# Low-rank update kernel: A read as 24 rows of 2 KB and transposed on the chip, A and B issued first from ScalarE's queue

## The chip, the cores and the metric

The kernel runs on one core of a Trainium2 chip. The core has five engines with their own instruction streams: TensorE (PE, matmuls; its weight loads are shown as PEld), VectorE (DVE), ScalarE (ACT), GpSimd (POOL) and SyncE (SP), which here only issues transfers. Sixteen DMA engines move data between the chip's main memory and the core's on-chip memory; they serve the queues of all engines that issue transfers. The metric is the device time of one execution in microseconds (us), a median over runs.

## The reference

```python
batch, seq, d_model, r = 16, 512, 768, 16      # x: 16 x 512 x 768, float32
lora = np.matmul(np.matmul(x, A), B)           # A: 768 x 16, B: 16 x 768
return (x + scale * lora).astype(np.float32)   # scale = 0.5
```

Seen as a matrix, x has 8192 rows of 768 floats (25.2 MB). All of it is read once and an output of the same size is written once. A and B are 48 KB each.

## The kernel before

The 8192 rows are cut into six parts, `PARTS = [2, 6, 8, 16, 16, 16]`, counted in sub-tiles of 128 rows. Part i has a tile of its own, `x_sb{i}`, and is loaded by one transfer (line 69); all six tiles fit on the chip together, so no load waits for room. The text calls these loads x0 to x5. After x1, the loop issues A (line 71) and B (line 72). All eight transfers, and later all eight stores (line 136), are issued by SyncE, so they stand in one queue.

A is laid out in memory as 768 rows of 16 floats. The kernel wants it with 128 rows on the 128 partitions, in six groups (`a_mm`, 128 x 6 x 16), so the load takes 768 pieces of 64 bytes. VectorE casts A and B to 16-bit floats (lines 75 and 77). GpSimd makes a 128 x 128 identity matrix.

The work goes by chunks of at most four sub-tiles, 17 in all. For a chunk:

- `transposed(c, j)`, for each of six column blocks j: TensorE transposes the sub-tiles with the identity (line 94) and ScalarE copies the result out of PSUM as 16-bit floats (line 96, `xt_sb`).
- `projected(c)`: six matmuls of `a_mm` with the transposed blocks add up to x times A, transposed (line 103); VectorE scales and casts it (line 108, `yt_sb`).
- `added(c, subs)`: for each sub-tile two matmuls with `b_mm` (line 120, `lora_ps`), and VectorE adds the result to x in place (line 126).
- `finished(c)`: once a part, or half of a part for the last two, is done, it is stored (line 136).

The main loop works on chunk c's transposes and chunk c-1's additions in turn. The framework plans the order of each engine's instructions at build time with its own estimate of durations and arrivals, so TensorE's order can differ from the program's; it also sets all waits. A transfer that reuses a tile's memory waits until the readers of what was there are done.

Of the kernel before, what the change touches and what calls it, by code (L numbers as in the profile page):

```python
# [1 line left out]

# [6 lines left out]


MM_DT = mybir.dt.float16

PARTS = [2, 6, 8, 16, 16, 16]

STORES = {4: [8, 8], 5: [8, 8]}

CHUNK = 4


@with_exitstack  # L20
def kernel(
    ctx: ExitStack,
    tc: tile.TileContext,
    x: bass.AP,
    A: bass.AP,
    B: bass.AP,
    scale: bass.AP,
    out: bass.AP,
):

    nc = tc.nc
    fp32 = mybir.dt.float32
    P = 128

    x2 = x.flatten_outer_dims()
    out2 = out.flatten_outer_dims()
    T, D = x2.shape
    R = A.shape[1]  # L40
    ND = D // P
    assert D % P == 0 and sum(PARTS) * P == T
    n_splits = [(n0, min(512, D - n0)) for n0 in range(0, D, 512)]
    sc = float(scale)

    const = ctx.enter_context(tc.tile_pool(name="const", bufs=1))
    xpool = ctx.enter_context(tc.tile_pool(name="xp", bufs=1))
    xtpool = ctx.enter_context(tc.tile_pool(name="xtp", bufs=6))
    ypool = ctx.enter_context(tc.tile_pool(name="yp", bufs=2))
    ps_xt = ctx.enter_context(tc.tile_pool(name="ps_xt", bufs=3, space=bass.MemoryType.PSUM))  # L50
    ps_y = ctx.enter_context(tc.tile_pool(name="ps_y", bufs=1, space=bass.MemoryType.PSUM))
    ps_l = ctx.enter_context(tc.tile_pool(name="ps_l", bufs=2, space=bass.MemoryType.PSUM))


    parts = []
    tok = 0
    for i, S in enumerate(PARTS):
        x_sb = xpool.tile([P, S, D], fp32, name=f"x_sb{i}")
        parts.append((x_sb, tok, S))
        tok += S * P  # L60

    def rows(t2, i):
        _, tok0, S = parts[i]
        return t2[ds(tok0, S * P), :].rearrange("(p s) d -> p s d", s=S)

    a_f32 = const.tile([P, ND, R], fp32, name="a_f32")
    b_f32 = const.tile([R, D], fp32, name="b_f32")
    for i in range(len(parts)):
        nc.sync.dma_start(out=parts[i][0], in_=rows(x2, i))  # L69
        if i == 1:  # L70
            nc.sync.dma_start(out=a_f32, in_=A.rearrange("(c p) r -> p c r", p=P))
            nc.sync.dma_start(out=b_f32, in_=B)

    a_mm = const.tile([P, ND, R], MM_DT, name="a_mm")
    nc.vector.tensor_copy(out=a_mm, in_=a_f32)  # L75
    b_mm = const.tile([R, D], MM_DT, name="b_mm")
    nc.vector.tensor_copy(out=b_mm, in_=b_f32)  # L77

    ident = const.tile([P, P], fp32, name="ident")
    make_identity(nc, ident)  # L80


    chunks = [
        (i, s0, min(CHUNK, S - s0))
        for i, (_, _, S) in enumerate(parts)
        for s0 in range(0, S, CHUNK)
    ]
    state = {}

    def transposed(c, j):  # L90
        i, s0, n = chunks[c]
        xt_ps = ps_xt.tile([P, CHUNK, P], fp32, name="xt_ps")
        for s in range(n):
            nc.tensor.transpose(xt_ps[:, s, :], parts[i][0][:, s0 + s, ds(j * P, P)], ident)  # L94
        xt_sb = xtpool.tile([P, CHUNK * P], MM_DT, name="xt_sb")
        nc.scalar.copy(out=xt_sb[:, 0 : n * P], in_=xt_ps[:, 0:n, :])  # L96
        state[c, j] = xt_sb

    def projected(c):
        n = chunks[c][2] * P  # L100
        ps_yt = ps_y.tile([R, CHUNK * P], fp32, name="ps_yt")
        for j in range(ND):
            nc.tensor.matmul(  # L103
                ps_yt[:, 0:n], a_mm[:, j, :], state.pop((c, j))[:, 0:n],
                start=(j == 0), stop=(j == ND - 1),
            )
        yt_sb = ypool.tile([R, CHUNK * P], MM_DT, name="yt_sb")
        nc.vector.tensor_scalar(  # L108
            out=yt_sb[:, 0:n], in0=ps_yt[:, 0:n], scalar1=sc, scalar2=None,
            op0=mybir.AluOpType.mult,  # L110
        )
        state[c] = yt_sb

    def added(c, subs):
        i, s0, n = chunks[c]
        subs = [s for s in subs if s < n]
        lora = {s: ps_l.tile([P, D], fp32, name="lora_ps") for s in subs}
        for s in subs:
            for n0, w in n_splits:
                nc.tensor.matmul(  # L120
                    lora[s][:, ds(n0, w)], state[c][:, ds(s * P, P)], b_mm[:, ds(n0, w)],
                    start=True, stop=True,
                )
        for s in subs:
            xs = parts[i][0][:, s0 + s, :]
            nc.vector.tensor_tensor(out=xs, in0=xs, in1=lora[s], op=mybir.AluOpType.add)  # L126

    def finished(c):
        i, s0, n = chunks[c]
        del state[c]  # L130
        end = 0
        for w in STORES.get(i, [parts[i][2]]):
            end += w
            if end == s0 + n:
                piece = slice(end - w, end)
                nc.sync.dma_start(out=rows(out2, i)[:, piece, :], in_=parts[i][0][:, piece, :])

    for c in range(len(chunks)):
        for j in range(3):
            transposed(c, j)  # L140
        if c >= 1:
            added(c - 1, (0, 1))
        for j in range(3, ND):
            transposed(c, j)
        if c >= 1:
            added(c - 1, (2, 3))
            finished(c - 1)
        projected(c)
    c = len(chunks) - 1
    added(c, (0, 1))  # L150
    added(c, (2, 3))
    finished(c)


# [1 line left out]
_INS = ['x', 'A', 'B', 'scale']  # L156
_OUTS = [((16, 512, 768), 'float32')]

_NUMBERS = {'scale': 0.5}


# [26 lines left out]
```

## Time and profile before

| | |
|---|---|
| median of three timings | 125.4 us (125.14, 125.40, 125.58) |
| span of the profiled execution, first to last instruction | 123.5 us |
| the profiled execution's own total | not given by the profile; 1.6 to 2.1 us of the timings lie around the span |
| TensorE busy | 98.0 us |
| VectorE busy | 68.5 us |
| ScalarE busy | 52.5 us |
| GpSimd busy | 0.7 us |
| data queue q1 | 50.43 MB, 16 DMA engines busy 96.4% of the span |
| last store issued | 111.40 us, landing 11.3 us later |

A transfer "lands" when the last of the 16 DMA engines has written its share. In tables by stretch of time, a DMA share of 1.00 means that each of the 16 engines had one packet under way all the time; it can be over 1, for packets overlap within an engine. A large packet counts in full where it is booked, so very short stretches swing widely, and stretches of several microseconds are the ones to read.

### The profile page before, as it was taken

The page shows a single profiled execution, that of the slowest core. Times are in us where ns is not written, and L with a number is a line of the kernel's source. Part 1 is how long each engine was busy: PE and PEld are TensorE (multiplying, and loading weights), DVE is VectorE, ACT ScalarE, POOL GpSimd, SP SyncE. Part 2 cuts the span into 40 slices and gives each one's busy share as a digit, 9 for nine tenths or more (in the row PEclk, how much of TensorE's full clock was granted, in tenths as well). Part 3 has the DMA queues.
Part 4 walks back from the last instruction along what each step waited for, and adds up shares of the span by engine and source line. Part 5 has one row for each costly group of instructions (what it writes and reads, how often), then busy time and mean ns, then how long its engine had stood idle before and what let it go on. Part 6 is the DMA issues. An engine that isn't in the chain of part 4 may idle for free.

```text
span 123.5 us, 1607 instructions
## 1 busy us (share of the span) xinstructions
PE 98.0 (79%) x614; PEld 61.0 (49%) x614; DVE 68.5 (55%) x83; ACT 52.5 (42%) x103; POOL 0.7 (1%) x6
## 2 busy tenths in 40 slices
PE   0263999999958999999999999999999999730000
PEld 0253665565616675656665665747475656200000
DVE  0000253962887267577686868686868576890000
ACT  4060364375504573737364555556473737000000
POOL 2000000000000000000000000000000000000000
PEclk9999999999999999999999999999999999995555
DMA  4999999799799899989799999989989999999990
GB/s 109 426 454 380 422 533 430 334 499 477 302 493 493 366 416 483 446 350 493 275 408 456 443 422 504 430 382 493 403 366 438 414 454 422 424 435 422 446 390 32
DMA packets 2840, 50.54 MB, mean 409 GB/s; under 512 B 1024, under 2 KB 1024, under 8 KB 1296
## 3 DMA queue, kind: packets, MB, share of 16 engines
q1 hardware_dynamic: 2832, 50.43, 96.4%
q8 instruction: 5, 0.08, 0.2%
q14 instruction: 3, 0.02, 0.0%
HBM read 25.26 MB, written 25.17 MB: 408 GB/s over the span
## 4 chain that ended last, share of the span: by engine, by line
PE 72%; DMA 8%; DVE 7%; issue 1%; DVEq 1%; SPq 0%; ACT 0%; ACTq 0%
PE xt_ps L94 38%; PE lora_ps L120 18%; PE ps_yt L103 16%; DMA x_sb<-in_x_dram 8%; DVE x_sb L126 6%; DVE yt_sb L108 1%; DVEq L183 1%; SPq L69 0%; ACT xt_sb L96 0%; ACTq L96 0%
## 5 line engine op out<-in xcount | busy, mean ns | idle before, releaser
L96 ACT CAST xt_sb<-xt_ps 128x512 f16<-128x512 f32 (+1 forms) x102 | 51.2, 568 | 52.0 <-PE xt_ps L94 47.2
L126 DVE TENSOR_TENSOR x_sb<-x_sb,lora_ps 128x768 f32<-128x768 f32 x64 | 58.0, 951 | 23.5 <-PE lora_ps L120 23.5
L94 PE MATMUL xt_ps<-ident,x_sb 128*128 128x128 f32 x384 | 52.3, 288 | 8.4 <-DMA x_sb<-in_x_dram 8.3
L94 PEld LDWEIGHTS xt_ps<-ident,x_sb 128*128 128x128 f32 x384 | 43.7, 146 | 20.7 <-issue 13.9
L120 PE MATMUL lora_ps<-b_mm,yt_sb 16*128 16x512 f16 (+1 forms) x128 | 26.7, 323 | 3.8 <-DVE x_sb L126 2.2
L103 PE MATMUL ps_yt<-xt_sb,a_mm 128*16 128x512 f16 (+1 forms) x102 | 24.4, 375 | 0.0
L120 PEld LDWEIGHTS <-yt_sb 16*128 16x128 f16 x128 | 9.5, 92 | 15.1 <-issue 7.8
L108 DVE TENSOR_SCALAR yt_sb<-ps_yt 16x512 f16<-16x512 f32 (+1 forms) x17 | 10.9, 642 | 8.0 <-PE ps_yt L103 8.0
L103 PEld LDWEIGHTS <-a_mm 128*16 128x16 f16 x102 | 7.9, 91 | 13.0 <-issue 5.1
L75 DVE CAST a_mm<-a_f 128x96 f16<-128x96 f32 x1 | 0.2, 210 | 11.4 <-DMA a_f<-in_A_dram 11.4
L96 ACT ACT_TABLE_LOAD x1 | 1.3, 1283 | 0.7 <-PEq L169 0.7
L77 DVE CAST b_mm<-b_f 16x768 f16<-16x768 f32 x1 | 0.5, 537 | 0.0
masks.py:199 POOL TENSOR_SCALAR_AFFINE_SELECT ident<-ident 128x128 f32<-128x128 f32 x1 | 0.3, 294 | 0.1
masks.py:197 POOL MEMSET ident<- 128x128 f32 x1 | 0.2, 205 | 0.3 <-POOLq L169 0.3
L169 POOL MEMSET const-bfloat16-1.0<- 128x1 bf16 x1 | 0.1, 103 | 0.0
L169 POOL MEMSET const-uint8-127<- 128x1 uint8 x1 | 0.1, 103 | 0.0
L169 POOL MEMSET const-float32-0.0<- 128x1 f32 x1 | 0.1, 100 | 0.2 <-issue 0.2
L169 POOL MEMSET const-float32-1.0<- 128x1 f32 x1 | 0.1, 100 | 0.0
## 6 DMA issues: line engine op xcount, KB each, us to landing
x_sb<-in_x_dram SPq DMA_DIRECT2D x3, 6144.0 KB, 45.1
out_dram<-x_sb SPq DMA_DIRECT2D x5, 3072.0 KB, 18.9
out_dram<-x_sb SPq DMA_DIRECT2D x1, 6144.0 KB, 27.6
x_sb<-in_x_dram SPq DMA_DIRECT2D x1, 3072.0 KB, 15.5
x_sb<-in_x_dram SPq DMA_DIRECT2D x1, 2304.0 KB, 9.8
out_dram<-x_sb SPq DMA_DIRECT2D x1, 2304.0 KB, 44.4
x_sb<-in_x_dram SPq DMA_DIRECT2D x1, 768.0 KB, 4.5
out_dram<-x_sb SPq DMA_DIRECT2D x1, 768.0 KB, 48.0
```

The source lines that it names most:

```text
L75: nc.vector.tensor_copy(out=a_mm, in_=a_f32)
L77: nc.vector.tensor_copy(out=b_mm, in_=b_f32)
L94: nc.tensor.transpose(xt_ps[:, s, :], parts[i][0][:, s0 + s, ds(j * P, P)], ident)
L96: nc.scalar.copy(out=xt_sb[:, 0 : n * P], in_=xt_ps[:, 0:n, :])
L103: nc.tensor.matmul(ps_yt[:, 0:n], a_mm[:, j, :], state.pop((c, j))[:, 0:n], start=(j == 0), stop=(j == ND - 1),)
L108: nc.vector.tensor_scalar(out=yt_sb[:, 0:n], in0=ps_yt[:, 0:n], scalar1=sc, scalar2=None, op0=mybir.AluOpType.mult,)
L120: nc.tensor.matmul(lora[s][:, ds(n0, w)], state[c][:, ds(s * P, P)], b_mm[:, ds(n0, w)], start=True, stop=True,)
L126: nc.vector.tensor_tensor(out=xs, in0=xs, in1=lora[s], op=mybir.AluOpType.add)
L169: nc = _bacc.Bacc("TRN2", target_bir_lowering=False, num_devices=1)
L183: with _tile.TileContext(nc) as tc:
```

## The change

A is read in its own order, as 24 rows of 32 x 16 floats (2 KB each), onto 24 partitions. VectorE then transposes it in blocks of 32 x 32, and four copies bring the blocks to the four groups of 32 partitions of `a_mm`, casting on the way. Because whole blocks of 32 are transposed, GpSimd first clears the 32 rows that the blocks are read from. A and B are issued from ScalarE's queue, ahead of its other work, while SyncE issues x0 to x4.

The rows of A, the transposed A and B's floats stand in a tile `room`, which has the size and the place of the last part's tile: `x_last` is allocated from the same slot. So x5's load is issued by SyncE after x4's, and waits until VectorE has read all that stands in `room`.

```diff
-    a_f32 = const.tile([P, ND, R], fp32, name="a_f32")
-    b_f32 = const.tile([R, D], fp32, name="b_f32")
-    for i in range(len(parts)):
+    def loaded(i):
+        S = parts[i][2]
+        parts[i][0] = xpool.tile([P, S, D], fp32, name=f"x_sb{i}")
         nc.sync.dma_start(out=parts[i][0], in_=rows(x2, i))
-        if i == 1:
-            nc.sync.dma_start(out=a_f32, in_=A.rearrange("(c p) r -> p c r", p=P))
-            nc.sync.dma_start(out=b_f32, in_=B)
-
+
+
+    last = len(parts) - 1
+    lastpool = ctx.enter_context(tc.tile_pool(name="lastp", bufs=1))
+    room = lastpool.tile([P, parts[last][2], D], fp32, name="room", tag="last")
+    NB = D // 32
+    a_rows = room[0:32, 0, 0 : 32 * R].rearrange("b (a r) -> b a r", r=R)
+    a_t = room[0:32, 1, 0 : 32 * R].rearrange("a (r b) -> a r b", r=R)
+    b_f32 = room[0:R, 2, :]
+    nc.gpsimd.memset(a_rows, 0.0)
+    nc.scalar.dma_start(out=a_rows[0:NB, :, :], in_=A.rearrange("(b a) r -> b a r", a=32))
+    nc.scalar.dma_start(out=b_f32, in_=B)
+    loaded(0)
+    loaded(1)
+    for i in range(2, last):
+        loaded(i)
+
+
+    nc.vector.transpose(out=a_t, in_=a_rows.rearrange("b a r -> b r a"))
     a_mm = const.tile([P, ND, R], MM_DT, name="a_mm")
-    nc.vector.tensor_copy(out=a_mm, in_=a_f32)
+    a_tv = a_t[:, :, 0:NB].rearrange("a r (c k) -> a k c r", k=4)
+    for k in range(4):
+        nc.vector.tensor_copy(out=a_mm[ds(32 * k, 32), :, :], in_=a_tv[:, k, :, :])
     b_mm = const.tile([R, D], MM_DT, name="b_mm")
     nc.vector.tensor_copy(out=b_mm, in_=b_f32)
+
+    parts[last][0] = lastpool.tile([P, parts[last][2], D], fp32, name="x_last", tag="last")
+    nc.sync.dma_start(out=parts[last][0], in_=rows(x2, last))
```

## The prediction

> **What bounds the kernel now.** I read the page first: busy shares, the DMA rows by slice, the DMA queues.
>
> ```profile
> span 123.5 us, 1607 instructions
> PE 98.0 (79%) x614; PEld 61.0 (49%) x614; DVE 68.5 (55%) x83; ACT 52.5 (42%) x103; POOL 0.7 (1%) x6
> DMA  4999999799799899989799999989989999999990
> DMA packets 2840, 50.54 MB, mean 409 GB/s; under 512 B 1024, under 2 KB 1024, under 8 KB 1296
> q1 hardware_dynamic: 2832, 50.43, 96.4%
> q8 instruction: 5, 0.08, 0.2%
> ```
>
> PE is busy 79% of the span, but the one data queue, q1, has the 16 DMA engines busy for 96.4% of it. The reader is to see that the DMA row never falls under 7 between the first slice and the last. 1024 packets are under 512 B: 768 are A's, one for each row of 16 floats (64 B), and the rest fit 16 completion marks for each of the 16 transfers.
>
> Next, the table by stretches (columns: stretch, its length, busy time and count of PE, PEld, DVE, ACT and POOL, granted clock, DMA share, GB/s).
>
> ```profile
> 0.70:1.70 1.00, 0.00 (x0) 0.00 (x0) 0.00 (x0) 0.96 (x1) 0.50 (x2) 1.00 0.00 0
> 1.70:4.00 2.30, 0.00 (x0) 0.00 (x0) 0.00 (x0) 0.32 (x1) 0.00 (x0) 1.00 0.98 323
> 4.00:9.50 5.50, 2.79 (x12) 2.39 (x12) 0.00 (x0) 2.23 (x6) 0.00 (x0) 1.00 1.02 430
> 9.50:11.50 2.00, 0.36 (x2) 0.39 (x3) 0.09 (x1) 0.00 (x0) 0.00 (x0) 1.00 1.18 375
> 62.00:100.00 38.00, 38.00 (x250) 23.71 (x249) 28.09 (x34) 20.56 (x40) 0.00 (x0) 1.00 1.01 433
> 110.00:120.00 10.00, 0.18 (x2) 0.00 (x0) 1.37 (x2) 0.00 (x0) 0.00 (x0) 0.57 0.99 428
> 120.00:121.00 1.00, 0.00 (x0) 0.00 (x0) 0.00 (x0) 0.00 (x0) 0.00 (x0) 0.50 0.46 197
> 121.00:122.00 1.00, 0.00 (x0) 0.00 (x0) 0.00 (x0) 0.00 (x0) 0.00 (x0) 0.50 0.06 25
> ```
>
> The rate is 428 to 433 GB/s whether loads or stores run, with PE busy or done. It is lower in the run-up to 4 us and in 9.5 to 11.5, where A's small packets pass: more busy time, fewer bytes.
>
> Third, issues with their times to landing, asked in short stretches of time so that single transfers show, and SyncE's timeline for when each was issued.
>
> ```profile
> x_sb<-in_x_dram SPq DMA_DIRECT2D x1, 2304.0 KB, 9.8
> x_sb<-in_x_dram SPq DMA_DIRECT2D x1, 3072.0 KB, 15.5
> x_sb<-in_x_dram SPq DMA_DIRECT2D x1, 6144.0 KB, 58.0
> out_dram<-x_sb SPq DMA_DIRECT2D x1, 768.0 KB, 48.0
> out_dram<-x_sb SPq DMA_DIRECT2D x1, 3072.0 KB, 14.6
> out_dram<-x_sb SPq DMA_DIRECT2D x1, 3072.0 KB, 11.3
> ```
>
> The queue is one line, first in, first out: the first store, issued at 18.34, lands at 66.3, just after the last load (issued 6.49, landing 64.5). The last two stores are issued at 100.86 and 111.40 and land at 115.46 and 122.70: 7.24 us apart, which is 3.146 MB at 434 GB/s. So the last store found the queue still busy and moved at full rate at once. The first load is issued at 0.74 and nothing moves before 1.70, so a transfer needs about 1.0 us to start; on the engines that end last the last store had 115.46 - 111.40 - 1.0 = 3.0 us to spare. The chain of waits shows PE for 72%, but that chain ends at 111.4; behind it come 11.3 us of queue. **The bound is the total work of the DMA queue; PE is second, 3.0 us behind it.**
>
> **The change, part by part.** The profile gives no total for its own execution beside the span of 123.5; the three timings are 125.14 to 125.58, median 125.4, so 1.6 to 2.1 us lie around the span. I sum against 123.5 and add 1.9.
>
> *A as 24 rows of 2 KB.* The same 49 KB of bytes, in 24 packets for 768. Upper bound, by busy time: 9.5 to 11.5 has 1.18 x 2.0 = 2.36 us of packets on the mean engine and moves 375 x 2.0 = 750 KB; the stretch before makes 430/1.02 = 422 GB/s for a full share, so these bytes are worth 1.78, and 0.58 us is the small packets' (0.58 x 16/768 = 12 ns each). Lower bound, by landings: x1 lands at 1.18 + 9.8 = 11.0 and x2 at 3.30 + 15.5 = 18.8, so x2, A and B (3.244 MB) took 7.8 us; at the 432 GB/s between the landings of the next two loads (6.291 MB from 34.9 to 49.45) that is 7.5, so 0.3 us is lost. The new packets cost at 12 ns each 24 x 12/16 = 0.02. Gain 0.3 to 0.56 us; I take 0.4, near the middle, because busy time counts overlap inside an engine and landings count the last engine alone. Everything else in the queue comes that much earlier, the end too.
>
> The Trainium skill, "DMA: Bandwidth & Descriptors", section "Why small descriptors are slow (HBM only)", has about 3 cycles of overhead per packet beside a beat per 32 B. At the page's 850 MHz that is, as an estimate, 48 packets x 5 cycles = 0.28 us for each engine, of which 0.11 are bytes: a gain of 0.17 and 125.2 us. The 12 ns above are about twice its 6 ns; I go by the trace.
>
> *B and A on ScalarE's queue.* SyncE issues 0.43 (A) and 1.14 (B) less, and x2 to x4 are issued earlier. The queue is already full then (share 1.02 from 4.0 to 9.5), so this is worth nothing; if the queue ran dry, it would be worth up to 1.57. B keeps its 16 packets, so it only moves ahead: 98 KB, 0.23 us, now share the engines with x0 or x1, which may land up to 0.23 later. PE waits for both of them (5.40 and 2.95 us of idle before its first transposes), so its start moves by this; the 3.0 us of spare time cover it.
>
> The Trainium skill, same page, "Issuing engines are not separate DMA queues", speaks against this part: all queues run on the same 16 engines, and only issue time is saved. By it the queue alone is worth 0 and the time would be 125.4. The trace has a single data queue and can't test it.
>
> *ScalarE.* A's issue waits for the memset: POOL is free at 0.73, and a 128-wide memset took 0.21, a 1-wide one 0.10, so 512 wide is some 0.5 (bounds 0.2 and 0.8): done at 1.25. With SyncE's rows of 0.43 and 1.14 ScalarE is through at 2.8; the table load (1.28) queued behind ends at 4.1. Its first cast starts at 6.10 now. Nothing; without that cover each us would delay the first casts, and so only PE's start.
>
> *POOL.* The identity comes 0.5 later, at 1.8; PE wants it at 5.4. Nothing.
>
> *VectorE.* Transpose 32x512: no row. From 0.21 (128x96 cast) to 0.95 (128x768 add); I take 0.54, the cast of 16x768. Four copies of 32x96 at no more than 0.21 each: 0.84; their gain over the one cast is none. B's cast 0.54 as now. Sum 1.9 us, in VectorE's idle time before 11.41. A's landing: issue at 1.25, plus 4.5 (x0's time to landing) to 9.8 (x1's), 5.8 to 11.1; I take 5.8, for A is small like x0 and early. a_mm is ready at 7.2, at worst 12.5; today projection starts at 12.59. Hidden.
>
> *The last load waits for room.* SyncE's sixth load stands behind VectorE's reads, until 7.8 to 13.0 in place of 6.49. What is queued behind it is the stores, the first at 18.34; the load before lands only at 49.45. Nothing, with over 30 us of cover.
>
> *PE.* With a_mm at 7.2, the first projection (six of 256 wide, 1.45) and the first result matmuls (0.82) can go into the idle 8.2 to 11.1. PE may be up to 2.3 us earlier, until it waits for x2 or x3. What is late next is the queue again: worth 0.
>
> Sum: 123.5 - 0.4 = 123.1, plus 1.9: **125.0 us**, 0.32% under the median.
>
> **Rivals.**
>
> *Hidden anyway.* The small packets overlap the big ones next to them (shares over 1 in that stretch say so), or a second queue costs back a little. For it: the lower bound is only 0.3. Against: fewer bytes did move. 125.1 to 125.5, say 125.3.
>
> *An engine that falls behind (slower).* The 16 engines don't end together: at 120 to 121 the share is 0.46, at 121 to 122 it is 0.06, and the last landing is 122.70. Five code loads (0.2% of 16 x 123.5, so 0.8 us each) each hold up one engine. The time is that of the last engine; if another order puts one more of these on it, 0.8 is lost: 125.4 - 0.4 + 0.8 = 125.8. It decides as soon as the extra load is worth more than 0.4. The reverse (the last engine is spared one) gives at most 0.8 less: 124.2. For it: code loads are there, and the program's instructions shift. Against: their number hardly changes.
>
> *PE's order.* The order of PE's instructions is planned at build time with A's arrival in view, and will be another. Now x3's first transposes start at 38.15, though x3 landed at 34.9. It decides when PE ends more than 3.0 us later than now; a further 1.0 makes 126.0 with the 0.4 gained. Against: early weights take work off PE, which gives it 2.3 more.
>
> **How the numbers follow.** Forecast 0.45; hidden 0.25; engine behind 0.14, engine spared 0.11; PE's order 0.05. A measurement of this kernel tells about 0.3% (0.38 us) from no change, so faster is under 125.02 and slower over 125.78. The forecast's own range is 124.8 to 125.2: about three quarters of its chance is under the bound with the timings' scatter, 0.33, plus 0.11 spared and 0.02 of hidden: 0.46 faster. Of engine behind and PE's order most is over, 0.16, and 0.04 for a cost around the span that the trace doesn't show: 0.20 slower. Same: 0.34. The range runs from 124.3 (spared, nearly whole) to 125.9 (engine behind, with scatter).
>
> **What would show it.** Right: under 512 B about 256 packets in place of 1024; no stretch at 375 GB/s near 10 us; x2 landing at about 18.4; a_mm written before 9 us; the last two stores' landings still 7.2 us apart, both about 0.4 earlier. Wrong: a gap of more than 7.3 us between these landings (PE then sets the end), a last engine further behind the others at 121 to 123, x0 or x1 landing over 0.3 later with no gain after, or a sixth load late enough for a slice of the DMA row to fall.

## The result and the profile after

The changed kernel takes 124.98 us in the median (124.79 to 125.64, 22 runs), the kernel before 125.41 us beside it: a ratio of 0.9964, with a 95% interval of 0.9947 to 0.9981. The prediction was 125.0. A second comparison gave 0.9948 (0.9918 to 0.9979). (Where runs are counted below, those that the comparison marked as disturbed are left out.) So the medians lie about 0.4 us apart. Where these come from is another matter, which the experiments take up.

The page after: busy shares, DMA row, packets, queues.

```profile
span 123.1 us, 1615 instructions
PE 97.8 (79%) x614; PEld 60.8 (49%) x614; DVE 70.3 (57%) x87; ACT 52.5 (43%) x103; POOL 1.1 (1%) x7
DMA  2999998999799699799799999989979999999981
DMA packets 2092, 50.54 MB, mean 410 GB/s; under 512 B 252, under 2 KB 252, under 8 KB 548
q1 hardware_dynamic: 2016, 50.33, 95.6%
q10 hardware_dynamic: 68, 0.10, 0.4%
```

The 768 small packets are gone (252 under 512 B for 1024), and a second data queue, q10, carries A and B. The DMA row is as full as before.

The stretches shown before, with the columns as there:

```profile
1.70:4.00 2.30, 0.00 (x0) 0.00 (x0) 0.00 (x0) 1.28 (x1) 0.05 (x1) 1.00 0.76 238
4.00:9.50 5.50, 3.25 (x15) 2.76 (x16) 2.51 (x6) 2.24 (x6) 0.00 (x0) 1.00 1.07 430
9.50:11.50 2.00, 0.92 (x5) 0.28 (x3) 0.41 (x1) 0.00 (x0) 0.00 (x0) 1.00 0.94 399
62.00:100.00 38.00, 38.00 (x248) 23.32 (x247) 28.09 (x34) 20.27 (x39) 0.00 (x0) 1.00 1.01 433
```

The dip at 9.5 to 11.5 is milder (375 before), but the start is worse: 238 GB/s for 323, which is (323 - 238) x 2.3 = 196 KB or 0.45 us at 432 GB/s.

The issues with their times to landing:

```profile
x_sb<-in_x_dram SPq DMA_DIRECT2D x1, 768.0 KB, 5.4
x_sb<-in_x_dram SPq DMA_DIRECT2D x1, 2304.0 KB, 10.5
x_sb<-in_x_dram SPq DMA_DIRECT2D x1, 3072.0 KB, 17.3
x_last<-in_x_dram SPq DMA_DIRECT2D x1, 6144.0 KB, 56.0
out_dram<-x_last SPq DMA_DIRECT2D x1, 3072.0 KB, 15.1
out_dram<-x_last SPq DMA_DIRECT2D x1, 3072.0 KB, 11.8
```

With the issue times of the trace (0.74, 1.17, 1.65, 8.17, 99.92, 110.46): x0 lands at 6.1, 0.9 us later than before; x1 at 11.6, 0.6 later; x2 at 18.95, about 0.1 later. Only x5 is earlier, 64.1 for 64.5, and from there on all is about 0.4 earlier: the last two stores land at 115.05 and 122.29, still 7.2 us apart. In this pair of profiles, then, what A's packets saved was spent by x2, and the gain arose later. One pair does not settle that: in a second profile of the changed kernel x2 lands at 18.5, 0.3 us earlier than before. Longer stretches of the first pair, the kernel before first, the changed one second:

```profile
1.70:14.00 12.30, 5.65 (x25) 4.22 (x25) 0.21 (x1) 3.14 (x8) 0.00 (x0) 1.00 1.02 396
14.00:56.00 42.00, 40.03 (x256) 25.06 (x256) 26.68 (x33) 21.35 (x44) 0.00 (x0) 1.00 1.02 437
56.00:70.00 14.00, 14.00 (x95) 8.85 (x93) 10.32 (x13) 7.98 (x16) 0.00 (x0) 1.00 0.96 396
70.00:110.00 40.00, 38.11 (x244) 22.88 (x242) 29.89 (x36) 19.02 (x37) 0.00 (x0) 1.00 1.01 431
```

```profile
1.70:14.00 12.30, 6.41 (x29) 5.31 (x30) 2.92 (x7) 4.32 (x9) 0.05 (x1) 1.00 0.98 392
14.00:56.00 42.00, 40.03 (x259) 24.42 (x258) 26.64 (x32) 21.57 (x44) 0.00 (x0) 1.00 1.01 433
56.00:70.00 14.00, 14.00 (x93) 8.59 (x92) 10.44 (x14) 7.82 (x15) 0.00 (x0) 1.00 1.00 426
70.00:110.00 40.00, 37.34 (x240) 22.51 (x237) 29.89 (x36) 18.76 (x36) 0.00 (x0) 1.00 1.00 431
```

Up to 14 us the changed kernel moves slightly less. At 56 to 70, where x5's last packets give way to the first stores, the kernel before falls to 396 GB/s and the changed one stays at 426. (Packets of 49 KB are booked whole, so the border at 56 is soft; 14 to 70 taken together is 427 against 431 GB/s, or 56 x 4/432 = 0.5 us. The border at 14 is soft too: there a packet has 24.6 KB, and one more or less on each of the 16 engines is 32 GB/s in the 12.3 us before and 7 GB/s in the 56 us behind. So these rates are a hint, and landings are the measure.)

### The profile page after: what moved, and what is told of

It reads as the page before. It is cut to its first block, busy times and chain, and to the rows that moved or that the text cites. A ratio compares the mean times of both kernels' runs of the same rounds, so it can differ in the third digit from the quotient of the medians.

```text
span 123.1 us, 1615 instructions
## 1 busy us (share of the span) xinstructions
PE 97.8 (79%) x614; PEld 60.8 (49%) x614; DVE 70.3 (57%) x87; ACT 52.5 (43%) x103; POOL 1.1 (1%) x7
## 4 chain that ended last, share of the span: by engine, by line
PE 71%; DMA 8%; DVE 7%; issue 1%; DVEq 1%; SPq 0%; ACT 0%; ACTq 0%
PE xt_ps L113 38%; PE lora_ps L139 18%; PE ps_yt L122 15%; DMA x_sb<-in_x_dram 8%; DVE x_last L145 3%; DVE x_sb L145 3%; DVE yt_sb L127 1%; DVEq L202 1%; SPq L68 0%; ACT xt_sb L115 0%; ACTq L115 0%
## 5 line engine op out<-in xcount | busy, mean ns | idle before, releaser
L145 DVE TENSOR_TENSOR x_sb<-x_sb,lora_ps 128x768 f32<-128x768 f32 x48 | 43.5, 950 | 21.2 <-PE lora_ps L139 21.2
L113 PE MATMUL xt_ps<-ident,x_sb 128*128 128x128 f32 x288 | 39.7, 290 | 7.7 <-DMA x_sb<-in_x_dram 7.6
L113 PEld LDWEIGHTS xt_ps<-ident,x_sb 128*128 128x128 f32 x288 | 33.1, 147 | 16.7 <-issue 11.5
L145 DVE TENSOR_TENSOR x_last<-x_last,lora_ps 128x768 f32<-128x768 f32 x16 | 14.5, 950 | 5.3 <-PE lora_ps L139 5.3
L113 PE MATMUL xt_ps<-ident,x_last 128*128 128x128 f32 x96 | 12.2, 277 | 0.0
L113 PEld LDWEIGHTS xt_ps<-ident,x_last 128*128 128x128 f32 x96 | 10.3, 140 | 3.0 <-PE ps_yt L122 1.7
L93 DVE CAST b_mm<-room 16x768 f16<-16x768 f32 x1 | 0.5, 548 | 4.4 <-DMA room<-in_B_dram 4.4
L87 DVE STREAM_TRANSPOSE room<-room 32x512 f32<-32x512 f32 x1 | 1.0, 1031 | 1.1 <-DMA room<-in_A_dram 1.1
L91 DVE CAST a_mm<-room 32x96 f16<-32x96 f32 x4 | 0.9, 232 | 0.1
L78 POOL MEMSET room<- 32x512 f32 x1 | 0.5, 515 | 0.3 <-POOLq L188 0.3
```

Of the source, the lines that this page charges most:

```text
L78: nc.gpsimd.memset(a_rows, 0.0)
L87: nc.vector.transpose(out=a_t, in_=a_rows.rearrange("b a r -> b r a"))
L91: nc.vector.tensor_copy(out=a_mm[ds(32 * k, 32), :, :], in_=a_tv[:, k, :, :])
```

## The experiments

Two questions were open: what A's packets, the place at the front and the second queue are each worth, and whether TensorE ever sets the end.

Four kernels take the change apart; the kernel before and the changed one were run again beside them. In the table, the ratio is to the kernel before in the same comparison, the two rates are GB/s in the profile.

| kernel | A's packets | issued by, where | median us | ratio (95%) | 1.7 to 14 | 14 to 70 |
|---|---|---|---|---|---|---|
| before, first profile | 768 | SyncE, after x1 | 125.41 | 1 | 396 | 427 |
| before again | 768 | SyncE, after x1 | 125.30 | 0.9996 (0.9956 to 1.0037) | 406 | 425 |
| rows in place | 24 | SyncE, after x1 | 125.07 | 0.9958 (0.9929 to 0.9987) | 412 | 428 |
| first from ScalarE | 768 | ScalarE, first | 125.10 | 0.9953 (0.9921 to 0.9984) | 392 | 430 |
| changed, no shared room | 24 | ScalarE, first | 124.98 | 0.9951 (0.9926 to 0.9977) | 396 | 430 |
| changed, again | 24 | ScalarE, first | 125.02 | 0.9948 (0.9918 to 0.9979) | 394 | 432 |
| front on one queue | 24 | SyncE, B, x0, A | 126.44 | 1.0055 (1.0015 to 1.0096) | 386 | 425 |

**The kernel before, again.**

> The kernel before once more, unchanged. In the first profile 0.45 us of queue work was lost between 58 and 62 us, where loads give way to stores (slow 48 KB packets), and not in the changed kernel. If this loss belongs to the kernel, the stretch 58 to 62 is again at about 385 GB/s; if it is chance, this profile has the full 430 there and its span is 123.0 to 123.2. Timing ratio to the kernel before: 1.000 +- 0.002.

The loss is there again: 391 GB/s from 56 to 70. (The 4 us that the expectation names are too short for packets booked whole: by the view used here they have 289 and 286 GB/s in the two profiles of the kernel before, 336 and 273 in those of the changed one.) Its span was 124.6, but for another reason, to which the last part of this section comes.

**A as rows, in A's old place.**

```diff
+    small = const.tile([P, D], fp32, name="small")
...
-            nc.sync.dma_start(out=a_f32, in_=A.rearrange("(c p) r -> p c r", p=P))
+            nc.sync.dma_start(out=a_rows[0:NB, :, :], in_=A.rearrange("(b a) r -> b a r", a=32))
...
+    nc.vector.transpose(out=a_t, in_=a_rows.rearrange("b a r -> b r a"))
```

> A as 24 rows of 2 KB with the on-chip transpose, but issued where A was, on SyncE after x1, and the last load in a tile of its own. Packet theory (768 small packets cost 0.3 to 0.56 us, the place of the issue nothing): same time as the changed kernel, ratio 0.996 to 0.997. Rival (the packets are worth 0.55 but going first from ScalarE costs 0.4 at the start): faster than the changed kernel by about 0.4, ratio 0.992 to 0.995, and 1.7 to 4.0 us again at 320 GB/s. Rival (the gain came from the stretch 58 to 62 because the last load waits): ratio 0.998 to 1.000.

0.9958: about the time of the changed kernel, as the packet theory has it. The gain sits where that theory puts it: 412 GB/s up to 14 us, the mean of the two profiles of before being 401. From 14 to 70 it is 428, as before. Landings agree: x2 is there at 18.56, and at 18.82 to 18.91 in the four profiles of kernels with the transfers of the kernel before.

**A in its 768 pieces, but A and B first from ScalarE.**

```diff
+    nc.scalar.dma_start(out=a_f32, in_=A.rearrange("(c p) r -> p c r", p=P))
+    nc.scalar.dma_start(out=b_f32, in_=B)
     for i in range(len(parts)):
         nc.sync.dma_start(out=parts[i][0], in_=rows(x2, i))
-        if i == 1:
-            nc.sync.dma_start(out=a_f32, in_=A.rearrange("(c p) r -> p c r", p=P))
-            nc.sync.dma_start(out=b_f32, in_=B)
```

> A in 768 pieces of 64 B as before, but A and B issued first from ScalarE. Packet theory: no change, ratio 1.000. Rival (going first costs 0.4 at the start): slower by 0.3 to 0.5 us, ratio 1.003, and under 250 GB/s from 1.7 to 4.0 us.

Both theories fail here: without a single packet less, the move alone gave 0.9953, and from 1.7 to 4.0 us it made 323 GB/s, as before, not under 250. Its profile does not show why it is faster. It fell on a long run (125.97 us), x2 lands at 19.02, 0.15 us later than before on average, and the last store but one at 115.28, where the kernel before has it (115.15 to 115.45 in the four profiles). None of its shorter runs was profiled, so whether the queue or an earlier TensorE gains there stays open.

**The changed kernel with A and B in a tile of their own.**

```diff
-    room = lastpool.tile([P, parts[last][2], D], fp32, name="room", tag="last")
-    a_rows = room[0:32, 0, 0 : 32 * R].rearrange("b (a r) -> b a r", r=R)
+    small = const.tile([P, D], fp32, name="small")
+    a_rows = small[32:64, 0 : 32 * R].rearrange("b (a r) -> b a r", r=R)
...
-    for i in range(2, last):
+    for i in range(2, last + 1):
         loaded(i)
```

> The changed kernel with A and B in a tile of their own, so that the last load is not held back. Packet theory: same time as the changed kernel, ratio 0.996 to 0.997. Rival (the last load's later issue spares the loss at 58 to 62): 0.3 to 0.45 us slower than the changed kernel, ratio 0.999 to 1.000, with 385 GB/s from 58 to 62.

0.9951, the changed kernel's time: that x5's load waits for room costs and brings nothing. The changed kernel run again was expected at 124.9 to 125.1, with at most one of 12 runs over 125.6 and at most 0.4 us lost from 56 to 70; it came to 125.02, with none, and to 427 GB/s there.

The ratios also hold the long runs of the kernel before, of which the last part of this section speaks. By runs up to 125.75 us alone, the medians of the comparison with these kernels are 125.32 before, 125.08 with rows in place, 125.07 with the pieces first from ScalarE and 124.98 with both. The kernel before run again has 125.18, so some 0.1 of such a difference is noise. Each half of the change is worth about 0.25 us by itself and both together 0.34: the halves do not add up.

**One queue, A and B at the front.**

```diff
-    nc.scalar.dma_start(out=a_rows[0:NB, :, :], in_=A.rearrange("(b a) r -> b a r", a=32))
-    nc.scalar.dma_start(out=b_f32, in_=B)
+    nc.sync.dma_start(out=b_f32, in_=B)
     loaded(0)
+    nc.sync.dma_start(out=a_rows[0:NB, :, :], in_=A.rearrange("(b a) r -> b a r", a=32))
```

> The changed kernel with B, x0 and A issued in this order on SyncE, so that there is one queue again but A and B stay at the front. If the second queue makes the gain: 125.2 to 125.3, with 0.5 us or more lost at 56 to 70 us. If the rows and the early weights make it: 124.9 to 125.1.

Slower than before, 1.0055, beyond what either side expected. With the same rows at nearly the same place, 1.4 us lie between it and the changed kernel. The order differs too, since A's issue waits for the memset and would have held up x0: A now stands between x0 and x1. So the run does not tell whether the single queue or A's place in it costs this. Its 16 engines drift apart: x1's share lands on the first engine at 10.7 and on the last at 12.8, in the changed kernel at 10.8 and 11.6, and the last landing is at 124.2, with the last store issued at 113.62.

**What the landings say.** The trace marks the landing of each transfer on each of the 16 engines. The mean of the 16 marks shifts less with one late engine than the last of them. In us from the start of the span, mean of the profiles, with lowest and highest (the kernels further below that change TensorE's work alone are counted with those whose transfers they have):

| A and B (profiles) | x2 | x5 | first store |
|---|---|---|---|
| pieces, SyncE after x1 (4) | 18.35 (18.25 to 18.40) | 62.63 (62.54 to 62.74) | 64.50 (64.41 to 64.62) |
| rows, SyncE after x1 (2) | 18.19 (18.16, 18.21) | 62.35 (62.27, 62.43) | 64.24 (64.15, 64.32) |
| pieces, ScalarE first (1) | 18.48 | 62.47 | 64.33 |
| rows, ScalarE first (4) | 18.40 (18.33 to 18.51) | 62.40 (62.37 to 62.43) | 64.25 (64.22 to 64.28) |
| rows, SyncE, B, x0, A (1) | 18.50 | 63.25 | 65.13 |

Rows after x1 are 0.17 us ahead of the pieces at x2 and 0.26 at the first store. Rows first from ScalarE are 0.05 behind at x2 but 0.25 ahead at the first store. The pages give x2's last landing, from its issue at 3.28 us (before again), 2.48 (rows in place) and 1.64 (changed, again):

```profile
x_sb<-in_x_dram SPq DMA_DIRECT2D x1, 3072.0 KB, 15.5
x_sb<-in_x_dram SPq DMA_DIRECT2D x1, 3072.0 KB, 16.1
x_sb<-in_x_dram SPq DMA_DIRECT2D x1, 3072.0 KB, 16.9
```

Going first, then, costs some 0.1 to 0.2 us by x2 in the mean of the engines, and the way from x2 to x5 is then 0.2 to 0.3 us shorter; with the rows the two cancel. With the pieces, in the one profile, 0.17 us are left. At the end it is the same: where the last store was not late, the last landing is at 122.70 and 122.52 with pieces on SyncE and at 122.21 to 122.32 in four profiles with rows in either place.

**The price of A's pieces by itself.** One more load behind B, of eight times A's bytes, once in pieces of 64 B and once in rows of 2 KB, into x5's tile, where x5 overwrites it.

```diff
+    x_last = parts[-1][0]
...
+            spare = x_last[:, 0, :].rearrange("p (c r) -> p c r", r=R)
+            nc.sync.dma_start(out=spare, in_=x2[0 : 48 * P, 0:R].rearrange("(c p) r -> p c r", p=P))
```

```diff
+    x_last = parts[-1][0]
...
+            spare = x_last[0:96, 0:2, 0:512]
+            nc.sync.dma_start(out=spare, in_=x2[0:192, 0:512].rearrange("(c p) r -> p c r", p=96))
```

> The kernel before with one more load behind B: 6144 pieces of 64 B of x (eight times A's 768), into the last part's tile, which x5's load overwrites later; its result is used for nothing. Packet theory at 12 ns each on 16 engines: 4.6 us of queue work more, by the lower bound 8 x (0.3 + 0.11) = 3.3 us; time 128.7 to 130.0. Rival (A's pieces cost hardly more than its bytes; what was lost at 10 us belongs to any small transfer there): 1.5 us or less, time under 127.

> The same bytes as in the run with 6144 pieces, in 192 rows of 2 KB. Both theories: 0.9 us for 393 KB and 0.14 for the packets, time about 126.5. The difference to 6144 pieces, divided by 8, is what A's pieces cost: 0.3 to 0.56 by the packet theory, 0.1 or less by its rival.

The stretch in which they move, pieces first, rows second:

```profile
9.00:16.50 7.50, 5.19 (x22) 3.71 (x23) 1.09 (x3) 1.76 (x3) 0.00 (x0) 1.00 1.21 218
```

```profile
9.00:16.50 7.50, 4.73 (x21) 3.58 (x21) 1.09 (x3) 1.44 (x3) 0.00 (x0) 1.00 1.04 358
```

(358 - 218) x 7.5 = 1050 KB less is moved, 2.4 us at 432 GB/s; divided by eight, A's pieces cost 0.30 us more than its rows. x2's landing says the same: 23.1 for 20.7. That is the lower bound of the prediction. (These pieces lie 3 KB apart in memory and A's side by side; whether that matters was not tested.) The times themselves (130.66 and 129.82) can't be used for this: in both TensorE was late and set the end, with the last store issued at 119.8 and 117.9, which the expectation for the rows missed by 3.3 us.

**TensorE as the second bound.** The profile of the kernel before, taken again, and that of the changed kernel, taken again, both caught a late clock. First the kernel before:

```profile
14.00:20.00 6.00, 6.00 (x24) 4.08 (x24) 2.70 (x4) 2.51 (x5) 0.00 (x0) 1.00 1.11 479
40.80:44.20 3.40, 3.40 (x19) 3.40 (x18) 0.75 (x1) 2.34 (x4) 0.00 (x0) 0.50 1.07 463
112.00:114.00 2.00, 1.47 (x4) 0.34 (x3) 1.98 (x3) 0.00 (x0) 0.00 (x0) 0.62 0.59 246
114.00:116.00 2.00, 0.11 (x1) 0.00 (x0) 1.10 (x2) 0.00 (x0) 0.00 (x0) 0.50 0.23 98
...
out_dram<-x_sb SPq DMA_DIRECT2D x1, 3072.0 KB, 8.7
```

TensorE does 24 matmuls between 14 and 20 us, 35 in the first profile, and later runs for 3.4 us at a granted clock of 0.50. The last store is issued at 115.13, not 111.40; the queue runs dry (246, then 98 GB/s), and the store lands 8.7 us after its issue. Now the changed kernel:

```profile
14.00:20.00 6.00, 6.00 (x25) 3.57 (x25) 1.98 (x3) 2.35 (x4) 0.00 (x0) 1.00 1.21 520
39.00:42.40 3.40, 3.40 (x18) 3.40 (x17) 0.99 (x2) 1.86 (x4) 0.00 (x0) 0.50 1.07 463
112.00:114.00 2.00, 0.24 (x2) 0.00 (x0) 1.44 (x2) 0.00 (x0) 0.00 (x0) 1.00 0.40 172
...
out_dram<-x_last SPq DMA_DIRECT2D x1, 3072.0 KB, 8.9
```

The same two delays, but the last store is out at 113.46 and lands at 122.3, where it also lands without them. The two executions took 126.42 and 125.03 us. In every profile of kernels with these transfers in which the last store came late (115.13, 114.69, 114.54, 114.34, 114.18) it landed 8.7 us after its issue. So the end is the later of two: the queue's own end, or the last store's issue plus 8.7. (In the long profile of the kernel with one queue at the front, with issue at 113.62 and landing at 124.2, it was the queue's.) They meet at 122.7 - 8.7 = 114.0 for the kernel before and at 122.3 - 8.7 = 113.6 after; TensorE has 2.6 us to spare in the first profile of the one and 3.1 in that of the other.

The timings fit: in the comparisons of the experiments 25 of 89 runs of the kernel before were over 125.75 us, and none of 34 of the changed one (highest 125.64). Without those 25 the median of the kernel before is 125.27, with them 125.36, and 125.00 after. Each run's mean granted clock is on record, and the long runs share a few values of it. All 15 runs at 0.938 or 0.939, the clock of the long profile above (0.938), took over 126.1 us, and all 12 at 0.925 took 125.59 or more; of the 62 others one was over 125.75. It is the course of the clock that tells, not its mean: the six runs at 0.908 and 0.909 took 125.25 to 125.70. Four runs were to test that TensorE's lateness makes the long ones.

Less work on TensorE, in the kernel before:

```diff
         for j in range(ND):
+            xt = state.pop((c, j))
+            if j == ND - 1:
+                continue
             nc.tensor.matmul(
...
```

> The kernel before with the last of the six projection matmuls of each chunk left out (so a sixth of x times A is missing): TensorE ends some 4 us earlier, the transfers are the same. Theory of two bounds (in about a third of the runs of the kernel before a stretch of lower granted clock makes TensorE late, the last store is issued after 113 us, and the queue runs dry): no run over 125.75, median 125.25. Theory of the queue alone: the same times as before, a third of them over 125.75, median 125.4.

It did not come out so: 5 of 9 runs were over 125.75, and their median is 125.78. With less to do TensorE was granted less: a mean clock of 0.89 to 0.91 in all its runs (0.91 to 0.95 in the kernel before beside it), and in the profile the last store was issued at 114.54. The run is no test of what the long ones come from, but fits in that TensorE's end decides: 114.54 + 8.7 = 123.2 is where the last store landed.

More work on TensorE, in the changed kernel:

```diff
+            xt = state.pop((c, j))
+            if j == 0 and 5 <= c < 9:
+                nc.tensor.matmul(ps_yt[:, 0:n], a_mm[:, 0, :], xt[:, 0:n], start=True, stop=True)
```

> The changed kernel with one projection matmul done twice in four of the chunks (the first is overwritten): four times 0.24 us more on TensorE, which puts the last store back to about 111.4 us, where the kernel before has it. Theory of two bounds: the fastest half stays at 124.8 to 125.0, but a fifth to a third of the runs are now over 125.6. Theory of the queue alone: no change, 124.98, all within 0.3.

124.94, with two of 12 runs over 125.6 (125.62 and 125.86). The profile fell on the former: last store issued at 114.34, span 123.8. The direction is as expected, but two of 12 against one of 34 settles nothing about how often.

TensorE kept busy from the start:

```diff
+    def warmed(n):
+        spare = ps_l.tile([P, D], fp32, name="lora_ps")
+        for s in range(n):
+            nc.tensor.transpose(spare[:, ds(s % 4 * P, P)], ident, ident)
...
+    warmed(16)
...
+        if c == 0:
+            warmed(12)
         projected(c)
```

> The kernel before with 28 transposes of the identity added on TensorE ahead of and between the first chunk's transposes, while it waits for x0 and x1; nothing reads them, and the transfers are the same. Theory of two bounds (the long runs of the kernel before are those where TensorE's clock came up late, at 20 us in place of 16, and fell again near 40): TensorE is warm before 12 us, the last store is issued at 109 to 111.5, at most 1 of 12 runs over 125.75, median 125.2 to 125.3, the queue's part unchanged. Theory of the queue alone: as the kernel before, median 125.4, a quarter to a third of the runs over 125.75.

> A as rows in place of the pieces, issued on SyncE after x1, with the 28 added transposes. Two bounds: the queue's gain of 0.25 and no long runs, median 124.9 to 125.0, as the changed kernel or 0.05 under it. If the queue on ScalarE is what gains: 125.2.

Both missed. The clock was up at 5.4 us, but TensorE idled again from 8.2 to 11.7, waiting for A, and fell back to 0.50 from 12.3 to 15.7 and once more near 40. In the kernel before, 4 of 12 runs stayed over 125.75 (median 125.47); with the rows the ratio was 0.9973 (0.9937 to 1.0008), and 125.39 the median of the nine runs that count, no better than rows alone, and the profile's last store was issued at 114.18. Here the early start of the clock was lost in the wait behind it. That TensorE's lateness makes the long runs is thus shown by profiles and fits the clocks on record; no run that takes it away shows it.

No kernel beats the changed one clearly; the one without shared room has the same time.

## Why the prediction was right, and where it was not

**The time** was right: 125.0 against 124.98, and in the first pair of profiles the last landing moved from 122.7 to 122.3, the 0.4 us that were forecast. It was met in part by luck: over all profiles the rows are worth 0.25 to 0.35 us of the queue, and about 0.1 of the difference between the medians goes with the long runs, which the prediction did not have. **The bound** was right for the profile that it was read from: the last two stores land 7.2 us apart, at full rate.

**"A as 24 rows of 2 KB"**: the size was near. The range was 0.3 to 0.56; the pair of extra loads gives 0.30, and the kernel with rows in place 0.26 by the landings and 0.24 by its runs. The 0.4 taken was too much; the landings were the better row, for the busy time counts overlap. The estimate from the Trainium skill ("DMA: Bandwidth & Descriptors", section "Why small descriptors are slow (HBM only)") was 0.17, too little by these runs.

**"Everything else in the queue comes that much earlier, the end too"** holds at the end, but not on the way there in the kernel as changed: averaged over the engines its x2 lands 0.05 us later than before, and only x5 and what follows 0.23 to 0.27 earlier. The step beside it, "B and A on ScalarE's queue ... worth nothing", is right as a sum for the rows (64.25 and 64.24 at the first store), but hides two effects of nearly equal size. At the front the rows and B put the last landing of x0 back by 0.4 to 0.9 us and that of x1 by 0.2 to 0.6, where the prediction had 0.23 at most; 0.1 to 0.2 of it is left at x2, and the prediction asked only what this does to PE's start, not to the queue. Of its own signs, x2's landing at about 18.4 was missed in the first profile (18.95) and nearly met in the three others with rows first from ScalarE (18.53 to 18.64). From x2 to x5, averaged over the engines, the five profiles with A and B on ScalarE then take 43.9 to 44.1 us, the six with A and B on SyncE after x1 44.1 to 44.4.

The Trainium skill's rule on issuing engines ("DMA: Bandwidth & Descriptors", section "Issuing engines are not separate DMA queues") gives the queue nothing but issue time. For the rows the landings agree with it in sum. The 768 pieces gained some 0.25 us of time by going first from ScalarE, and the rows at the front of one queue took 126.44 us against 125.02 on two; but in both the place changed with the queue, so these runs differ from the rule without showing that the queue is the reason. Why the stretch where loads give way to stores is slower with SyncE's queue alone stays open. It was so in all seven profiles of kernels whose only small loads are A and B on SyncE (383 to 398 GB/s from 56 to 70, against 402 to 427 in the five with ScalarE), but the profile with 192 more rows on SyncE had 412.

**ScalarE, POOL, the last load**: right. The memset took 0.52 us, ScalarE's issues (B's first, for A's waited) and table load ended at 3.1, x5's load was issued at 8.17 and cost nothing, as the kernel without shared room shows.

**VectorE** was mis-sized and stayed hidden: the transpose took 1.03 us, over its upper bound of 0.95 (0.54 taken), the copies 0.23 each for 0.21. A was there at 6.1 (5.8 taken), a_mm at 8.1 for 7.2, still before the first projection at 9.0.

**TensorE "may be up to 2.3 us earlier ... worth 0"**: the last store is issued 0.94 us earlier (110.46 for 111.40). Worth 0 in the profiles in which TensorE was on time, as said, but not where the clock makes it late: there 1.4 us lay between two such executions (126.42 and 125.03). The prediction read one profile in which the clock held and took 3.0 us of cover for safe; it was 2.6, and more than a quarter of the runs were long. Of the 0.36 us between the medians of these 89 and 34 runs (125.36 and 125.00) about 0.09 goes with the long runs, of the 0.54 between their means (125.56 and 125.02) 0.29.

**The rivals.** "Hidden anyway" was wrong: the last landing is 0.2 to 0.5 us earlier with rows, in either place. "An engine that falls behind" did not decide for the changed kernel; in the profile of its neighbour with one queue it did. "PE's order" did no harm.

## What to carry to other kernels

Where a transfer queue is full from start to end, count its work by landings, over all engines and several profiles, and not by busy time or by the rates of stretches whose borders cut packets. Treat a small transfer's place and queue as a change of its own: here the packets were worth 0.25 to 0.3 us, the new place and queue next to nothing on top of that, and one kernel with the same rows at the front of a single queue was slower than before. Beside a saturated queue, ask how far behind the second bound is in a bad execution, not in the profiled one. The spread in the timings before (124.8 to 126.8) was the sign here that two bounds take turns.

## What the runs showed of the hardware

TensorE's granted clock fell to 0.50 for 3.4 or 6.8 us in every profile of the experiments, mostly near 40 us. It came up to stay, until then, between 14 and 21 us, in the same kernel at different times (15.8 and 20.3 us in the two profiles of the kernel before, with 35 and 24 matmuls from 14 to 20 us). The Trainium skill, "TensorE: Matmul & The Clock Gate", section "What's actually happening", has a free-running window of 3413 ns and two states; the 3.4 us and 0.50 here agree. Leaving out work did not help TensorE: with a sixth of the projections gone it ran at a lower mean clock (0.89 to 0.91), and in its profile the last store was issued at 114.54, between the two profiles of the kernel before (111.40 and 115.13).

A 3 MB store into a queue that had run nearly dry landed 8.7 us after its issue in seven profiles, so some 1.4 us come on top of the 7.2 to 7.3 us that lie between the landings of two such stores when the queue is full.
